# A top-256 search with eight rounds instead of nine, and both ends of its interval in one tile

## The chip, the core and the metric

The kernel runs on one core of one Trainium2 chip. The core has five engines that run side by side, each through its own fixed list of instructions: PE (TensorE, matmuls), DVE (VectorE), ACT (ScalarE), POOL (GpSimd) and SP (SyncE, which here issues the DMA transfers). The metric is the device time of one execution in microseconds (us); lower is better. The time before is the median of three runs, 2610.61 us (2607.62 to 2613.69).

## The reference

One decoder layer on 2048 tokens of width 1024. What matters here is how each query chooses its keys: an indexer scores all earlier positions, the 256 best are kept, and attention runs over these alone.

```python
rel = jax.nn.relu(jnp.einsum('bqhd,bsd->bqhs', qi_b.astype(jnp.float32), ki32))
score = jnp.einsum('bqhs,bqh->bqs', rel, w_b.astype(jnp.float32))
causal = key_pos[None, :] <= t_b[:, None]
score = jnp.where(causal[None], score, NEG_INF)
_, sel = lax.top_k(score, k_sel)
valid = sel <= t_b[None, :, None]
...
logits = jnp.where(valid[:, None], logits, NEG_INF)
p = jax.nn.softmax(logits, axis=-1).astype(v.dtype)
```

Around it stand one input projection, a short gated convolution (y = B * conv3(C * h)), RMS norms, one output projection, layer norms, and a SwiGLU feed-forward of width 2816.

## The kernel before, in words

The 2048 tokens are 16 blocks of 128. Blocks 0 and 1 have at most 256 earlier positions, so they take all; blocks 2 to 15 each need a threshold per query. The kernel finds it without sorting, in `topk`: it keeps an interval from `lo` to `hi` around the threshold of each query, guesses `t` inside it, counts how many scores are at or above `t`, and lets the count replace one end. `NITER` rounds of this bring the upper end to where between 248 and 255 scores lie above it; then one pass masks these, `V.max` takes the eight largest of the rest, and the missing rank picks the threshold (L549 to L555). The last pass (L559) writes the 0/1 mask `u` and counts it into `flag`. If any query's count is not exactly 256, a branch at the end of attention runs the general path: `general_topk` (31 bitwise rounds for every block) and attention once more.

A round is: for each block of the group, ACT counts the last `n2` columns with a sign activation (L507) and DVE counts the rest with a comparison that accumulates (L509); then small DVE instructions of 2 to 8 elements a row join the counts (L512), decide which end moves (L513 to L516), and interpolate the next `t` (L519 to L534; L536 to L541 are special steps of rounds 2 and 3). Counts and thresholds lie side by side in one tile `tcur`, as they do in `lo` and `hi`, so one predicated copy moves both.

The searches run in five groups. Blocks (2,3,4,5), (6,7,8) and (9,10) are the early ones. Their steps are interleaved with the scoring of further blocks (`weighted`, L454), with the projections, the convolution (`conv`, L732 on PE) and the weights of the adaLN modulation (L266). A group's search starts only when the group before it has ended. Scores of all blocks are written to memory (`s_d`). When scoring is over and the third search has ended, the memory it held is given to attention: query loads (`qst`, L838), scaled output weights (`wr`, L812), and the tile `scb` into which scores of the late groups (11,12,13) and (14,15) are loaded back. The late searches then run in the background of attention: one step of them in each step of attention. Attention takes blocks in the order 2, 4, 7, 0, 10, 1, 9, 3, 8, 5, 6, 11, 13, 12, 15, 14. For each block DVE first finds the largest logit per query and head (`maxima`: matmul L858, L860 on DVE, transpose L870 on PE), then PE makes logits (L883 to L885), ACT exponentials (L889, L890), GpSimd a rest (L891), and PE multiplies with the values (L901 to L903). GpSimd computes nothing in the front but small copies and memsets: the convolution's two-column halo (L740, L742) and the constants `zero` and `below`.

Every engine's list is fixed when the program is built: a scheduler orders the instructions by priority and by its own estimate of when each could start.

Of the kernel before, what the change touches and what calls it, by code (L numbers as in the profile page):

```python
# [11 lines left out]
F32 = mybir.dt.float32  # L12
F16 = mybir.dt.float16
BF16 = mybir.dt.bfloat16
I32 = mybir.dt.int32
AF = mybir.ActivationFunctionType
ALU = mybir.AluOpType
# [4 lines left out]
P = 128  # L22
# [29 lines left out]


TGT = 252.0
NITER = 9
CLIP = 0.04
PROBE = 2
DVE_SHARE = 0.42
# [67 lines left out]
def rsqrt(V, pool, dst, src, eps):  # L126
    n = dst.shape[1]
    v = pool.tile([P, n], F32, tag=f"rv{n}", name="rv", bufs=2)
    y = pool.tile([P, n], F32, tag=f"ry{n}", name="ry", bufs=2)
    a = pool.tile([P, n], F32, tag=f"rw{n}", name="rw", bufs=2)  # L130
    i = pool.tile([P, n], I32, tag=f"ri{n}", name="ri", bufs=2)
    V.tensor_scalar(v, src, eps, None, op0=ALU.add)
    V.tensor_scalar(i, v.bitcast(I32), 1, None, op0=ALU.logical_shift_right)
    V.tensor_scalar(y.bitcast(I32), i, -1.0, float(0x5F3759DF), op0=ALU.mult, op1=ALU.add)
    V.tensor_scalar(v, v, -0.5, None, op0=ALU.mult)
    for k in range(3):
        V.tensor_tensor(a, y, y, op=ALU.mult)
        V.tensor_tensor(a, a, v, op=ALU.mult)
        V.scalar_tensor_tensor(dst if k == 2 else y, a, 1.5, y, op0=ALU.add, op1=ALU.mult)
# [3 lines left out]
def body(ctx: ExitStack, tc: tile.TileContext, A, out, force=False):  # L143
    nc = tc.nc
    V, S_, G, T = nc.vector, nc.scalar, nc.gpsimd, nc.tensor
# [182 lines left out]
    for q in range(4):  # L328
# [5 lines left out]
        for b, ps in first.items():  # L334
            hi, lo = hts[b // 4]
# [18 lines left out]
    tk = tks.enter_context(tc.tile_pool(name="tk", bufs=1, side="right", reuse_waits="tile"))  # L354
# [103 lines left out]
    def topk(blocks, scs):  # L458
        nb = len(blocks)
        b0 = blocks[0]  # L460

        def sm(name, k=1):
            return tk.tile([P, k, nb], F32, tag=f"{name}", name=f"{name}{b0}", bufs=2)

        def cst(c):
            return ct[:, c + b0:c + b0 + nb]

        st6 = tk.tile([P, nb, 6], F32, tag="st6", name=f"st6_{b0}")
        mv = tk.tile([P, nb, 2], F32, tag="mv", name=f"mv_{b0}")
        for i in range(nb):  # L470
            m = 2 * TOPK if blocks[i] >= 4 else TOPK
            head = tk.tile([P, 2 * TOPK], F32, tag="sp", name="head")[:, 0:m]
            S_.activation(head, scs[i][:, 0:m], AF.Copy, scale=1.0 / SS2)
            V.bn_stats(st6[:, i], head)
            V.bn_aggr(mv[:, i], st6[:, i])
            yield
        mu, sd = sm("mu")[:, 0], sm("sd")[:, 0]
        rsqrt(V, tk, sd, mv[:, :, 1], 1e-30)
        V.scalar_tensor_tensor(sd, sd, SS2, mv[:, :, 1], op0=ALU.mult, op1=ALU.mult)
        V.tensor_scalar(mu, mv[:, :, 0], SS2, None, op0=ALU.mult)  # L480
        tcur, lo, hi = sm("tc", 2), sm("lo", 2), sm("hi", 2)
        a, f = sm("a")[:, 0], sm("f")[:, 0]
        big, nbig = sm("big"), sm("nbig")
        cd, ca2 = sm("cd")[:, 0], sm("ca2")[:, 0]
        t = tcur[:, 0]
        cnt = tcur[:, 1]
        V.tensor_tensor(a, sd, cst(C_Z), op=ALU.mult)
        V.tensor_tensor(t, a, mu, op=ALU.add)
        V.scalar_tensor_tensor(lo[:, 0], sd, -6.0, mu, op0=ALU.mult, op1=ALU.add)
        V.scalar_tensor_tensor(hi[:, 0], sd, 8.0, mu, op0=ALU.mult, op1=ALU.add)  # L490
        zero, below = sm("zero")[:, 0], sm("below")[:, 0]

        n2 = int(sum(b + 1 for b in blocks) / nb * P * (1 - DVE_SHARE)) // 64 * 64
        big_at, tgt = TOPK - n2 / 2.0, TGT - n2 / 2.0
        V.tensor_scalar(lo[:, 1], cst(C_N), -n2 / 2.0, None, op0=ALU.add)
        V.memset(hi[:, 1], -n2 / 2.0)
        G.memset(zero, 0.0)
        G.memset(below, -2100.0)
        dd = sm("dd", 2)
        yield  # L500
        for it in range(NITER):
            for i, b in enumerate(blocks):
                n = (b + 1) * P
                n1 = n - n2
                j1 = tk.tile([P, 1024], BF16, tag="j1", name="j1", bufs=1)
                j2 = tk.tile([P, 1216], BF16, tag="j2", name="j2", bufs=1)
                S_.activation(j2[:, 0:n2], scs[i][:, n1:n], AF.Sign, bias=t[:, i:i + 1],  # L507
                              scale=-1.0, accum_out=ca2[:, i:i + 1])
                V.tensor_scalar(j1[:, 0:n1], scs[i][:, 0:n1], t[:, i:i + 1], None,  # L509
                                op0=ALU.is_ge, op1=ALU.add, accum_out=cd[:, i:i + 1])  # L510
                yield
            V.scalar_tensor_tensor(cnt, ca2, -0.5, cd, op0=ALU.mult, op1=ALU.add)  # L512
            V.tensor_scalar(big[:, 0], cnt, big_at, None, op0=ALU.is_ge)  # L513
            V.tensor_scalar(nbig[:, 0], cnt, big_at, None, op0=ALU.is_lt)
            V.copy_predicated(lo, big.bitcast(I32).broadcast_to([P, 2, nb]), tcur)
            V.copy_predicated(hi, nbig.bitcast(I32).broadcast_to([P, 2, nb]), tcur)  # L516
            if it == NITER - 1:
                break
            V.tensor_tensor(dd, hi, lo, op=ALU.subtract)  # L519
            d = dd[:, 0]  # L520
            if it == 0:
                V.scalar_tensor_tensor(a, cnt, -tgt, sd, op0=ALU.add, op1=ALU.mult)
                V.tensor_tensor(a, a, cst(C_SL), op=ALU.mult)
                V.tensor_tensor(a, a, t, op=ALU.add)
                V.scalar_tensor_tensor(f, d, 0.02, lo[:, 0], op0=ALU.mult, op1=ALU.add)
                V.tensor_tensor(a, a, f, op=ALU.max)
                V.scalar_tensor_tensor(f, d, -0.02, hi[:, 0], op0=ALU.mult, op1=ALU.add)
                V.tensor_tensor(t, a, f, op=ALU.min)
            else:
                V.reciprocal(a, dd[:, 1])  # L530
                V.scalar_tensor_tensor(f, lo[:, 1], -tgt, a, op0=ALU.add, op1=ALU.mult)
                V.tensor_scalar(f, f, CLIP - 1.0, -CLIP, op0=ALU.max, op1=ALU.min)
                V.tensor_tensor(f, f, d, op=ALU.mult)
                V.tensor_tensor(t, lo[:, 0], f, op=ALU.subtract)  # L534
            if it == PROBE:
                V.tensor_scalar(a, lo[:, 0], 0.0, None, op0=ALU.is_lt)  # L536
                V.scalar_tensor_tensor(f, hi[:, 0], 0.0, a, op0=ALU.is_gt, op1=ALU.mult)
                V.copy_predicated(t, f.bitcast(I32), zero)
            if it == PROBE + 1:
                V.tensor_scalar(f, hi[:, 0], 0.0, None, op0=ALU.is_equal)  # L540
                V.copy_predicated(t, f.bitcast(I32), below)  # L541
            yield
        r, thr, m8 = sm("rk")[:, 0], sm("thr")[:, 0], tk.tile([P, nb, 8], F32, tag="m8", name=f"m8{b0}")
        ri = tk.tile([P, nb], I32, tag="ri_", name=f"ri{b0}")
        V.tensor_scalar(ri, hi[:, 1], n2 / 2.0 + 0.25, None, op0=ALU.add)
        V.tensor_scalar(r, ri, -1.0, float(TOPK), op0=ALU.mult, op1=ALU.add)
        for i, b in enumerate(blocks):
            n = (b + 1) * P
            sp = tk.tile([P, S], F32, tag="sp", name="sp", bufs=1)  # L549
            V.tensor_scalar(sp[:, 0:n], scs[i], hi[:, 0, i:i + 1], 2.0 * NEG, op0=ALU.is_ge, op1=ALU.mult)  # L550
            V.tensor_tensor(sp[:, 0:n], sp[:, 0:n], scs[i], op=ALU.add)
            yield
            V.max(m8[:, i], sp[:, 0:n])
            pick = tk.tile([P, 8], F32, tag="pick", name="pick")
            V.scalar_tensor_tensor(pick, ct[:, C_IOTA:C_IOTA + 8], r[:, i:i + 1], m8[:, i], op0=ALU.is_equal,  # L555
                                   op1=ALU.mult, accum_out=thr[:, i:i + 1])
            yield
            u = tk.tile([P, S], BF16, tag="u", name="u", bufs=1)
            V.tensor_scalar(u[:, 0:n], scs[i], thr[:, i:i + 1], None, op0=ALU.is_lt, op1=ALU.add,  # L559
                            accum_out=flag[:, b:b + 1])  # L560
            S_.activation(u[:, 0:n], u[:, 0:n], AF.Copy, scale=NEG)
            dma(u_d[b - 2], u[:, 0:n])
            yield
# [1065 lines left out]
```

## Time and profile before

| | before |
|---|---|
| median of three runs | 2610.61 us |
| the profiled execution, time | 2611.21 us |
| its span | 2609.4 us |
| PE busy | 2346.9 us (90%) |
| DVE busy | 1868.2 us (72%) |
| ACT busy | 1197.2 us (46%) |
| POOL busy | 1179.2 us (45%) |
| mean granted PE clock | 0.952 |

The shares are means over stages that differ. Up to about 590 us the kernel projects, scores, convolves and runs the early searches; from there to about 1310 us it attends, with the late searches up to about 900 us; behind it the feed-forward, where PE is nearly always busy. What an edit to the search is worth has to be read from the first two stages.

### The profile page before, as it was taken

The page shows a single profiled execution, that of the slowest core. Times are in us where ns is not written, and L with a number is a line of the kernel's source. Part 1 is how long each engine was busy: PE and PEld are TensorE (multiplying, and loading weights), DVE is VectorE, ACT ScalarE, POOL GpSimd, SP SyncE. Part 2 cuts the span into 40 slices and gives each one's busy share as a digit, 9 for nine tenths or more (in the row PEclk, how much of TensorE's full clock was granted, in tenths as well). Part 3 has the DMA queues.
Part 4 walks back from the last instruction along what each step waited for, and adds up shares of the span by engine and source line. Part 5 has one row for each costly group of instructions (what it writes and reads, how often), then busy time and mean ns, then how long its engine had stood idle before and what let it go on. Part 6 is the DMA issues. An engine that isn't in the chain of part 4 may idle for free. (4 is left out here: it accounts for less than half of the span.)

```text
span 2609.4 us, 38313 instructions
## 1 busy us (share of the span) xinstructions
PE 2346.9 (90%) x13538; PEld 1128.6 (43%) x13538; DVE 1868.2 (72%) x3812; ACT 1197.2 (46%) x2291; POOL 1179.2 (45%) x950
## 2 busy tenths in 40 slices
PE   6799999895787889989969999999999996999998
PEld 3444444342443445545524444444444442344443
DVE  8998999989998977775268776666666787422223
ACT  3687767555676655757733332333323343110000
POOL 3000000004453564676636655655556664855445
PEclk8899999997898989999989999999999997999999
DMA  7421442415121142330133222222222236444443
GB/s 265 129 99 68 147 135 90 148 57 188 47 97 63 64 147 71 112 127 30 67 122 121 85 69 81 73 77 85 78 84 85 89 101 195 150 137 146 134 133 122
DMA packets 213913, 281.69 MB, mean 108 GB/s; under 512 B 15824, under 2 KB 128848, under 8 KB 212944
## 3 DMA queue, kind: packets, MB, share of 16 engines
q1 hardware_dynamic: 213712, 279.17, 33.7%
q8 instruction: 107, 1.75, 0.3%
q14 instruction: 94, 0.77, 0.1%
HBM read 183.20 MB, written 95.91 MB: 107 GB/s over the span
## 5 line engine op out<-in xcount | busy, mean ns | idle before, releaser
L1201 PE MATMUL f<-h,wwg 128*128 128x512 f16 x1800 | 419.0, 383 | 24.5 <-ACT h L1164 18.1
L891 POOL TENSOR_TENSOR pr<-p,ph 128x512 f16<-128x512 f32 x272 | 326.2, 1218 | 222.9 <-ACT ph L890 147.6
L1201 PE MATMUL f<-h,wwu 128*128 128x512 f16 x1800 | 413.4, 379 | 0.0
L1497 PEld LDWEIGHTS <-gi 128*128 128x128 f16 x1848 | 181.6, 99 | 276.7 <-DMA gi<-gg_d 46.3
L1235 POOL TENSOR_TENSOR go<-g,go 128x512 f16<-128x512 f32 x126 | 169.6, 1356 | 275.3 <-ACT go L1234 233.6
L1201 PEld LDWEIGHTS <-wwg 128*128 128x128 f16 x1848 | 181.9, 99 | 231.3 <-issue 13.7
L1201 PEld LDWEIGHTS <-wwu 128*128 128x128 f16 x1848 | 180.8, 98 | 233.1 <-issue 15.6
L1497 PE MATMUL f<-wdo,gi 128*128 128x512 f16 x1032 | 243.2, 388 | 15.3 <-DMA gi<-gg_d 8.5
L860 DVE CUSTOM_DVE_ANT_0 jk<-m,ua 128x512 bf16<-128x512 f32 (+3 forms) x320 | 193.9, 606 | 64.6 <-PE m L858 49.7
L889 ACT ACTIVATE p<-l 128x512 f32<-128x512 f32 x272 | 157.6, 597 | 87.2 <-PE l L885 77.4
L1234 ACT ACTIVATE go<-g 128x512 f16<-128x512 f32 x132 | 82.7, 628 | 231.6 <-issue 82.8
L447 ACT ACTIVATE r<-xs 128x512 f32<-128x512 f32 (+3 forms) x304 | 154.0, 549 | 60.8 <-PE xs L446 16.6
L890 ACT ACTIVATE ph<-p 128x512 f16<-128x512 f32 x272 | 166.1, 633 | 3.3 <-PE o L903 0.8
L1497 PE MATMUL f<-wdr,gi 128*128 128x512 f16 x576 | 137.1, 387 | 14.4 <-DMA gi<-gg_d 14.4
L732 PE MATMUL b<-hi,wch 128*128 128x512 f16 x384 | 147.0, 383 | 1.2 <-ACT g L737 1.2
L732 PE MATMUL b<-lo,wch 128*128 128x512 f16 x384 | 146.8, 382 | 0.0
L732 PE MATMUL b<-hi,wcl 128*128 128x512 f16 x384 | 146.3, 381 | 0.0
L903 PE MATMUL o<-vst,pr 128*128 128x65 f16 x1088 | 136.9, 198 | 6.8 <-POOL pr L891 6.4
L901 PE MATMUL o<-vst,ph 128*128 128x65 f16 x1088 | 140.1, 196 | 1.2 <-ACT ph L890 1.0
L902 PE MATMUL o<-vst,ph 128*128 128x64 f16 x1088 | 139.5, 196 | 0.0
L858 PE MATMUL m<-k1T,qst 128*128 128x512 f16 (+3 forms) x320 | 110.1, 376 | 32.1 <-DVE mp L860 26.1
L1464 ACT ACTIVATE frs<-fmv,epsw 128x1 f32<-128x1 f32 x16 | 4.7, 295 | 283.3 <-DVE fmv L1461 283.3
(384 smaller groups left out, 5319.8 us busy)
## 6 DMA issues: line engine op xcount, KB each, us to landing
gg_d<-go SPq DMA_DIRECT2D x154, 256.0 KB, 2.6
gi<-gg_d SPq DMA_DIRECT2D x112, 256.0 KB, 3.0
wa<-in_w_ada SPq DMA_DIRECT2D x64, 256.0 KB, 2.9
wg<-in_wg SPq DMA_DIRECT2D x49, 256.0 KB, 3.0
wu<-in_wu SPq DMA_DIRECT2D x49, 256.0 KB, 3.0
wd<-in_wd SPq DMA_DIRECT2D x44, 256.0 KB, 2.9
gi<-gg_d SPq DMA_DIRECT2D x56, 192.0 KB, 2.8
wa<-in_w_ada SPq DMA_DIRECT2D x16, 512.0 KB, 8.6
```

The lines of the kernel that those rows point to most:

```text
L447: S_.activation(r[:, i:i + e], ps[:, 0:e], AF.Relu)
L732: T.matmul(ps, w[:, k, j * P:(j + 1) * P], x[:, k], start=n == 0, stop=n == 3 * KT - 1)
L860: V.tensor_tensor_reduce(jk[:, 0:w], ps[:, 0:w], u[:, j * 512:j * 512 + w], scale=1.0, scalar=-3e38, op0=ALU.add, op1=ALU.max, accum_out=m ...
L889: S_.activation(p32, pl_, AF.Exp, scale=DH ** -0.5)
L890: S_.activation(ph, p32, AF.Copy)
L891: G.tensor_tensor(pr, p32, ph, op=ALU.subtract)
L901: T.matmul(o, lhs, vst[:, kt, 64:129], start=kt == 0 and hh == 0, stop=False)
L902: T.matmul(o[:, 0:64], lhs, vst[:, kt, 0:64], start=False, stop=False)
L903: T.matmul(o, pr[:, hh * P:(hh + 1) * P], vst[:, kt, 64:129], start=False, stop=kt == b and hh == 3)
L1201: T.matmul(ps, w[:, x, k * P:(k + 1) * P], h[:, y, :, k], start=n == 0, stop=n == 11)
L1235: (V if (p, grp) in LASTG else G).tensor_tensor(o[:, :, 1], x4, o[:, :, 0], op=ALU.subtract)
L1497: T.matmul(ps, g[:, p - p0, x], wd_tiles[m, p][:, y], start=p == 0 and n == 0, stop=p == NP - 1 and n == 2)
```

## The change

`NITER` goes from 9 to 8. `lo` and `hi` become two halves of one tile `ends`. Where two comparisons made the predicates `big` and `nbig` and two predicated copies moved `lo` and `hi`, one comparison now makes both predicates at once (the count is at or above the goal, compared with a constant row of 0 for `lo` and of 1 for `hi`), and one predicated copy moves whichever end it is. The constant tile `upper` is written by two GpSimd memsets at the start of each group.

```diff
-NITER = 9
+NITER = 8
...
-        tcur, lo, hi = sm("tc", 2), sm("lo", 2), sm("hi", 2)
+        tcur = sm("tc", 2)
+
+        ends = tk.tile([P, 2, 2, nb], F32, tag="ends", name=f"ends{b0}", bufs=2)
+        lo, hi = ends[:, 0], ends[:, 1]
         a, f = sm("a")[:, 0], sm("f")[:, 0]
-        big, nbig = sm("big"), sm("nbig")
+        which, upper = sm("which", 2), sm("upper", 2)
...
+        G.memset(upper[:, 0], 0.0)
+        G.memset(upper[:, 1], 1.0)
...
             V.scalar_tensor_tensor(cnt, ca2, -0.5, cd, op0=ALU.mult, op1=ALU.add)
-            V.tensor_scalar(big[:, 0], cnt, big_at, None, op0=ALU.is_ge)
-            V.tensor_scalar(nbig[:, 0], cnt, big_at, None, op0=ALU.is_lt)
-            V.copy_predicated(lo, big.bitcast(I32).broadcast_to([P, 2, nb]), tcur)
-            V.copy_predicated(hi, nbig.bitcast(I32).broadcast_to([P, 2, nb]), tcur)
+            V.scalar_tensor_tensor(which, tcur[:, 1:2].broadcast_to([P, 2, nb]), big_at, upper,
+                                   op0=ALU.is_ge, op1=ALU.not_equal)
+            V.copy_predicated(ends, which.bitcast(I32).unsqueeze(2).broadcast_to([P, 2, 2, nb]),
+                              tcur.unsqueeze(1).broadcast_to([P, 2, 2, nb]))
```

The change also moves other instructions, since the scheduler orders anew. Three places, where a name with a number is one buffer of that tile, and where L517 to L524 of the changed kernel are L512 to L519 of the one before, L737 is L732, L817 is L812, and L863 and L865 are L858 and L860.

DVE, one of the last rounds of the third search, before:

```order
L512 SCALAR_TENSOR_TENSOR tc_3300<-ca_3308,cd_3307 128x2
L513 TENSOR_SCALAR big_3305<-tc_3300 128x2
L514 TENSOR_SCALAR nbig_3306<-tc_3300 128x2
L515 COPY_PREDICATED lo_3301<-big_3305,tc_3300 128x4
L516 COPY_PREDICATED hi_3302<-nbig_3306,tc_3300 128x4
L519 TENSOR_TENSOR dd_3319<-hi_3302,lo_3301 128x4
L530 RECIPROCAL a_3303<-dd_3319 128x2
```

and now:

```order
L517 SCALAR_TENSOR_TENSOR tc_3127<-ca_3134,cd_3133 128x2
L518 SCALAR_TENSOR_TENSOR which_3131<-tc_3127,upper_3132 128x4
L520 COPY_PREDICATED ends_3128<-which_3131,tc_3127 128x8
L524 TENSOR_TENSOR dd_3147<-ends_3128 128x4
L535 RECIPROCAL a_3129<-dd_3147 128x2
```

Four instructions became two; each of the five now needs the result of the one ahead of it. In all, DVE has 149 instructions fewer.

DVE, the end of scoring (`scl` are scores of blocks 11 to 15, L620 is the last step of scoring, `ada` the adaLN weights), before:

```order
L454 SCALAR_TENSOR_TENSOR scl_3934<-r,wis,scl_3934 128x1024
L755 TENSOR_TENSOR y<-y,g 128x512
L475 BN_AGGR mv_3251<-st_9_3250 128x2
L620 TENSOR_TENSOR scl_3934<-scl_3934,ct 128x128
L132 TENSOR_SCALAR rv<-mv_3251 128x2
```

and now:

```order
L514 TENSOR_SCALAR j_3153,cd_3133<-sc_2399,tc_3127 128x512
L266 SCALAR_TENSOR_TENSOR ada_6043<-wa,ca,ada_6043 128x512
L751 SCALAR_TENSOR_TENSOR y<-u,pp,y 128x512
L454 SCALAR_TENSOR_TENSOR scl_3820<-r,wis,scl_3820 128x1024
L514 TENSOR_SCALAR j_3226,cd_3133<-sc_2399,tc_3127 128x640
L753 SCALAR_TENSOR_TENSOR y<-b,y 128x512
```

The head of the third search and the counts of its first round (L514 of the changed kernel) moved ahead of the last scores; before, they stood behind them. From the last score to the search's last instruction there are 189 DVE rows before and 128 now.

PE, the seam between convolution and attention, before:

```order
L732 LDWEIGHTS wcl_5974
L732 MATMUL b<-hi_1062,wcl_5974 128x512
L858 LDWEIGHTS qst_6674
L858 MATMUL m<-k1T,qst_6674 128x384
```

and now:

```order
L737 LDWEIGHTS wch_5859
L737 MATMUL b<-lo_1063,wch_5859 128x512
L863 LDWEIGHTS qst_6560
L863 MATMUL m<-k1T,qst_6560 128x384
...
L737 LDWEIGHTS wcl_5860
L737 MATMUL b<-hi_1062,wcl_5860 128x512
```

Before, the convolution's last matmul stands ahead of the first matmul of attention. Now 67 convolution matmuls stand behind that first one, mixed with the maxima of the first block.

## Rows read from the trace of the kernel before

**Rows 1.** Stretches: busy us (count) of PE, PEld, DVE, ACT, POOL; PE clock.

```profile
183.00:590.00 407.00, 392.35 (x1865) 181.76 (x1863) 380.00 (x985) 270.89 (x550) 20.27 (x41) 0.99 0.33 106
590.00:900.00 310.00, 232.22 (x1923) 123.08 (x1922) 293.28 (x822) 202.36 (x399) 135.24 (x116) 0.87 0.27 93
...
480.00:520.00 40.00, 33.38 (x138) 14.10 (x136) 39.65 (x79) 21.25 (x35) 2.95 (x4) 0.96 0.42 138
520.00:580.00 60.00, 60.00 (x269) 27.15 (x268) 53.56 (x176) 30.19 (x55) 1.52 (x10) 1.00 0.15 45
580.00:600.00 20.00, 11.11 (x49) 4.67 (x47) 14.92 (x33) 7.61 (x11) 0.19 (x1) 0.90 0.86 297
```

**Rows 2.** Waits of PE, 590 to 900 us: total us, times, longest.

```profile
PE m L858 <- DVE mp L860: 19.4, 29, 2.2
PE m L870 <- DVE mx L866: 16.4, 4, 6.2
```

**Rows 3.** Waits of DVE, 590 to 900 us.

```profile
DVE jk L860 <- PE m L858: 5.3, 5, 1.8
```

**Rows 4.** Waits of PE, 183 to 590 us.

```profile
PE xs L446 <- ACT r L447: 6.2, 6, 2.0
PE b L752 <- ACT g L749: 5.8, 3, 4.3
```

**Rows 5.** The chain that ended last, its first pieces: start, us, what.

```profile
1336.38 4.46 PE f L1201 x12
```

**Rows 6.** Line L509 alone by stretch: length, DVE busy us (count), PE clock.

```profile
183.00:590.00 407.00, 50.69 (x162) 0.99 0.33 106
590.00:900.00 310.00, 46.33 (x90) 0.87 0.27 93
```

**Rows 7.** Tile `big` (L513 and L515) by stretch, columns as before.

```profile
183.00:590.00 407.00, 9.10 (x54) 0.99 0.33 106
590.00:900.00 310.00, 9.69 (x36) 0.87 0.27 93
```

**Rows 8.** Tile `nbig` (L514 and L516) by stretch.

```profile
183.00:590.00 407.00, 8.85 (x54) 0.99 0.33 106
590.00:900.00 310.00, 9.58 (x36) 0.87 0.27 93
```

**Rows 9.** Timeline of DVE, a round of the third search: start, us, instruction.

```profile
557.58 0.16 DVE L512 SCALAR_TENSOR_TENSOR tc<-ca,cd 128x2 f32<-128x2 f32 x1 [0.41 <-ACT j L507]
557.78 0.17 DVE L513 TENSOR_SCALAR big<-tc 128x2 f32<-128x2 f32 x1
557.86 0.16 DVE L514 TENSOR_SCALAR nbig<-tc 128x2 f32<-128x2 f32 x1
...
558.45 0.17 DVE L530 RECIPROCAL a<-dd 128x2 f32<-128x2 f32 x1
558.65 0.16 DVE L531 SCALAR_TENSOR_TENSOR f<-lo,a 128x2 f32<-128x2 f32 x1
...
559.45 0.75 DVE L509 TENSOR_SCALAR_CACHE_REDUCE j<-sc,tc 128x512 bf16<-128x512 f32 x1
560.12 0.09 DVE L509 DVE_READ_ACCUMULATOR j<-sc,tc 128x1 f32 x1
...
561.96 0.16 DVE L512 SCALAR_TENSOR_TENSOR tc<-ca,cd 128x2 f32<-128x2 f32 x1 [0.84 <-ACT j L507]
```

**Rows 10.** Timeline of DVE: scoring's end, the third search's first round, its end.

```profile
512.55 0.28 DVE L620 TENSOR_TENSOR scl<-scl,ct 128x128 f32<-128x128 f32 x1
...
521.80 0.15 DVE L512 SCALAR_TENSOR_TENSOR tc<-ca,cd 128x2 f32<-128x2 f32 x1
...
583.20 0.08 DVE L559 DVE_READ_ACCUMULATOR u<-sc,thr 128x1 f32 x1
```

**Rows 11.** Timeline of SP's queue and PE at the seam.

```profile
582.28 0.63 SPq L838 DMA_DIRECT2D qst<-q_d  x1
...
587.37 0.81 PE L858 MATMUL m<-k1T,qst 128*128 128x384 f16 x4
...
600.54 0.40 PE L870 MATMUL m<-ct,mx 128*72 128x128 f32 x1 [8.44 <-DVE mv L475]
```

**Rows 12.** Line L515: ns min/median/max, first and last start, forms.

```profile
L515 DVE COPY_PREDICATED lo<-big,tc x45: 152/167/1134, 193.5 to 885.3; 128x6 f32<-128x6 int32 x18, 128x4 f32<-128x4 int32 x18, 128x8 f32<-128x8 int32 x9
```

## The prediction

> **What bounds the kernel now.** Start with the table of stretches [rows 1], because the change touches only 183 to 900 us and a mean over the whole kernel hides two regimes. From 183 to 590 us (projections, scores, convolution, and the three early searches) PE is busy 392.4 of 407 us and DVE 380.0: both are nearly full. From 590 to 900 us (attention with the two late searches in its background) DVE is busy 293.3 of 310 us, PE only 232.2, and PE's granted clock is down to 0.87. Next come the waits: between 590 and 900 us PE's longest are for the maxima that DVE takes [rows 2], while DVE waits for PE only 5.3 us [rows 3]. So DVE sets the pace there. In the front PE waits 12.0 us for two results of ACT [rows 4], and by the code each of them follows a DVE step (L454, L748). The chain that ended last begins at 1336 us [rows 5], after all this, so it can't price the change. I use it for one thing: it is made of work and of loads that follow work, so what is won before it is kept as a shift.
>
> **One search round on DVE.** The timeline of the last early search shows a bare round: 561.96 - 557.58 = 4.38 us from one L512 to the next [rows 9]. Instructions that depend on each other start 0.20 us apart; independent neighbours start 0.08 us apart although each is recorded with 0.16. So a small instruction takes 0.075 us of DVE when other work fills the gaps, and up to 0.20 when nothing does.
>
> **Term 1, the count passes.** Their line, accumulator reads included, is busy 50.7 us in the front and 46.3 us behind it, over nine rounds [rows 6]. One round of all early groups is 5.6 us, of all late groups 5.1 us; less the overlap in the records (0.07 us for 9 and 5 passes) 5.0 and 4.8 us. ACT loses its part of the count too; it is busy 202 of 310 us in the late stretch [rows 1], so that is worth nothing by itself.
>
> **Term 2, the small instructions.** A removed round takes eleven with it. Each of the remaining rounds (24 early, 16 late) loses two: L513 to L516 become one comparison and one predicated copy. In the front the four lines are busy 9.10 + 8.85 us [rows 7, 8], 0.166 each, none waiting. Late they are 9.69 + 9.58 us for only 72, 0.27 each. The Trainium skill, "SBUF — State Buffer", section "SBUF: two separate sides", says that DVE and GpSimd share a port pair as an exclusive lock which a DVE instruction with two SBUF inputs, or in a two-port mode, waits for. That agrees with 0.166 against 0.27, and it speaks against part of the change: the new comparison reads two SBUF tiles where the old ones read one, so the waits might only move to it; by that the late saving is the lower end below.
>
> Late round removed: eleven small ones at 0.075 (all hidden) to 0.27 each; I take 0.18, or 2.0 us a group, 4.0 for both groups (1.6 to 5.9). With the passes 8.8 us (6.4 to 10.7). Two instructions fewer in 16 rounds: 2.4 us at 0.075; at the measured late mean 0.54 a round less 0.17 of overlap, 5.9 us. I take 4, since a GpSimd instruction that no longer meets L515 may meet the next one. Late sum on DVE 12.8 us (8.8 to 16.6). DVE is busy 95% of that stretch, so I turn 0.9 of it into time: **11.5 us**, ends 7 and 16.6.
>
> **Term 3, the front up to the end of scoring (183 to 512 us).** Groups (2,3,4,5) and (6,7,8) lose a round each: 3.4 us of passes and 2 x 0.83 of small ones; two instructions in 16 rounds at 0.075 are 2.4 us: 7.5 us of DVE. But the order of the changed kernel moves work in: the head of the third search and its first round now stand ahead of the last score, about 27 small instructions, two BN_STATS and two passes, 4.7 us of DVE. What is left is 2.8 us. PE has little to win: 6.6 us idle from 480 to 520 us, where DVE is at 39.65 of 40 [rows 1]. I take **3 us**, between 0 (PE is the bound) and 7 (the crunch at 480 to 520 goes). The two new memsets per group go to GpSimd, idle here 387 of 407 us [rows 1]. The halo copies that the convolution needs (L740, L742) queue behind them. They wait for nothing: the buffer is that of the group two before, whose search has ended. So I cost them at nothing; if one did wait, a halo copy and with it PE would wait as long.
>
> **Term 4, the seam at 583 to 600 us.** Attention's first loads wait for the memory that the third search holds. Before: scoring ends at 512.55, the search's last instruction is at 583.20 [rows 10], the first query load is issued at 582.28, PE starts the first maxima at 587.37, when the last convolution matmul is in, and then stands idle 8.44 us until 600.54 [rows 11]. From 580 to 600 us DVE is idle 5.1 us and PE 8.9 [rows 1]. After: from the end of scoring to the end of the search there are 128 DVE rows instead of 189. In time that is 70.7 us, less a round of 4.4, less 0.8 for the two instructions in seven rounds, less 9.3 (512.55 to 521.80, head and first round, now earlier [rows 10]): about 56 us, so the search ends 14.5 us earlier against the convolution, whose PE work is unchanged. The order agrees: the first maxima matmul now stands 67 convolution matmuls before their end, and at 60.0/269 us each [rows 1] that is 14.9 us. The burst of loads and the first maxima then run beside convolution. DVE's own saving here is 3.0 us for the round and 0.8; to that come the idle time at the seam (up to 5.1), and the 6.4 us that DVE is idle from 520 to 580 [rows 1], of which the 14 us window can refill only a part. I take **10 us**; the ends are 4 (own work alone) and 15 (all of it).
>
> **Sum.** 11.5 + 3 + 10 = 24.5 us. Against the profiled execution of 2611.2 us (its span is 2609.4) that gives 2586.7; the median of the runs shown is 0.6 us lower, so 2586. The ends together: 7 + 0 + 4 = 11 and 16.6 + 7 + 15 = 38.6, hence 2600 and 2572.
>
> **Rivals.** *PE takes over.* With the maxima earlier, PE's own work could become the bound in part of 590 to 900 us and keep half of the gain, 2599. For it: 232 us of matmuls at a granted clock of 0.87. Against it: some 36 us of its idle time (19.4 and 16.4) name DVE's maxima alone [rows 2].
>
> *The seam backfires.* PE runs in order, and 67 convolution matmuls now queue behind the first maxima. If the search ends as late against the convolution as before, PE stands still for up to 14.9 us and convolution with it: 24.5 less the seam's 10 and 14.9 more lost, 2611. It decides when u of the last block lands later than PE's arrival there. Against it: the 14.5 us above, worked out without that order, cover it.
>
> *The wide copy is dear (slower).* No row shows a predicated copy with both its inputs broadcast, on up to 16 elements. The nearest, L515, has 0.167 us as its median for 4, 6 and 8 elements alike, and 1.13 us at its longest [rows 12]. If every one of the 40 new copies cost that longest, they would take 40 x 0.97 = 39 us more on DVE, and the time would be 2586 + 39 = 2625. It decides at 0.61 us more per copy (24.5/40). The equal medians for three sizes speak against it.
>
> *Eight rounds don't settle a row.* Then the flag (L559) sends the kernel through the general path: 31 passes over 17,024 columns at 0.75/512 us each [rows 9], 770 us, and attention a second time, some 700 us (590 us to the chain's start at 1336 [rows 5] bounds it): about 4,060 us. A single row of the 1,792 decides. Following the search's arithmetic in single precision on the reference's inputs, one row is open after seven rounds, none after eight or nine; so this is remote, though the margin is one round.
>
> **How the numbers follow.** Forecast 0.68; PE takes over 0.16; the seam backfires 0.06; dear copy 0.04; general path 0.02; more than my upper ends (PE's clock rises as its gaps close, 0.87 in the late stretch) 0.04. The range 2568 to 2603 holds the forecast with its ends, PE taking over, and a little of the last; it leaves out about 2 in 10 with the tails of each. A measurement of this kernel can tell about 0.2%, 5.2 us, from no change. Faster by more than that: 0.68 + 0.16 + 0.04 and some of the seam case, 0.89. Within it: 0.05, most of the seam case. Slower: 0.06.
>
> **What would show it.** The profile after should have 112 passes on the count line instead of 126 and 149 DVE instructions fewer; 590 to about 876 us with DVE still near 95%; the third search ending at least 10 us before the last convolution matmul; no PE wait of 8 us at the first transpose of maxima; everything behind 1000 us shifted by one constant. I am wrong if the new copy is recorded above 0.3 us in the front, if PE idles inside the convolution for the first query tile, or if DVE's share from 590 to 900 us drops while the time does not.

## The result and the profile after

The changed kernel takes **2589.45 us** (median of four runs, 2585.36 to 2590.99) against 2609.11 us for the kernel before beside it: a ratio of 0.9916 [0.9903, 0.993], 20 to 22 us faster. The profiled execution is the shortest of its four, 2585.36 us, 25.9 us below the profiled 2611.21 of before. So the forecast of 2586 held in its sum. It did not hold in its parts, and most of what follows is about that.

First the stretches of the kernel after, with the columns of [rows 1]: length, busy us (count) of PE, PEld (PE's weight loads), DVE, ACT, POOL, then PE's granted clock, the DMA share and GB/s.

```profile
183.00:590.00 407.00, 392.09 (x1871) 182.27 (x1869) 382.81 (x927) 269.16 (x543) 22.54 (x50) 0.98 0.37 119
590.00:900.00 310.00, 236.84 (x1882) 124.99 (x1883) 287.58 (x753) 202.09 (x398) 151.62 (x122) 0.86 0.28 93
...
480.00:520.00 40.00, 40.00 (x179) 18.16 (x178) 37.74 (x82) 22.13 (x41) 3.08 (x4) 1.00 0.48 154
520.00:580.00 60.00, 60.00 (x274) 27.37 (x273) 51.26 (x139) 29.35 (x49) 1.64 (x12) 1.00 0.36 128
580.00:600.00 20.00, 9.09 (x29) 3.30 (x28) 19.00 (x48) 9.04 (x15) 3.54 (x4) 0.72 0.29 93
```

PE's idle time at the end of scoring is gone: from 480 to 520 us it is busy 40.0 us where it was busy 33.38 [rows 1]. From 590 to 900 us DVE is 5.7 us less busy, PE 4.6 us more. At the seam, 580 to 600 us, PE is busy 9.09 us, less than the 11.11 of [rows 1].

PE's waits from 590 to 900 us (total us, times, longest), which answer to [rows 2]:

```profile
PE m L863 <- DVE mp L865: 20.3, 23, 2.2
PE l L888 <- ACT p L894: 14.0, 15, 4.6
PE m L964 <- DVE z L956: 12.2, 4, 4.7
PE m L875 <- DVE mx L871: 8.8, 4, 3.2
```

The wait for the transposed maxima fell from 16.4 to 8.8 us; the one for the single maxima stayed (19.4, now 20.3).

The seam in the timelines of DVE, SP's queue and PE (start, us, instruction, idle before), answering to [rows 10, 11]:

```profile
559.53 0.08 DVE L564 DVE_READ_ACCUMULATOR u<-sc,thr 128x1 f32 x1
...
555.46 1.08 SPq L843 DMA_DIRECT2D qst<-q_d  x1
...
582.00 0.38 PE L737 MATMUL b<-hi,wcl 128*128 128x512 f16 x1
583.60 0.22 PE L863 MATMUL m<-k1T,qst 128*128 128x128 f16 x1 [1.23 <-ACT pc L877]
587.64 0.59 PE L863 MATMUL m<-k1T,qst 128*128 128x512 f16 x1 [3.83 <-DVE mp L865]
589.32 0.27 PE L863 MATMUL m<-k1T,qst 128*128 128x128 f16 x1 [1.09 <-DVE mp L865]
591.25 2.08 PE L757 MATMUL b<-g,ct 128*128 128x512 f32 x2 [1.66 <-ACT g L754]
```

The third search ends at 559.53, 23.7 us earlier than the 583.20 of [rows 10], and 22 us ahead of the last convolution matmul at 582.00. Query loads are issued at 555.46 instead of 582.28 [rows 11]. The single wait of 8.44 us is gone, but several of 1 to 4 us stand in its place.

What was saved on DVE, by line and stretch (length, DVE busy us, count): the count passes L514, answering to [rows 6], and the new pair, L518 and L520, answering to [rows 7, 8] (tile `which`).

```profile
183.00:590.00 407.00, 44.81 (x144) 0.98 0.37 119
590.00:900.00 310.00, 41.13 (x80) 0.86 0.28 93
...
183.00:590.00 407.00, 7.92 (x48) 0.98 0.37 119
590.00:900.00 310.00, 10.76 (x32) 0.86 0.28 93
...
L520 DVE COPY_PREDICATED ends<-which,tc x40: 158/170/1087, 193.3 to 830.8; 128x12 f32<-128x12 int32 x16, 128x8 f32<-128x8 int32 x16, 128x16 f32<-128x16 int32 x8
```

There are 72 + 40 = 112 passes (their accumulator reads double the count in the rows), as forecast. The new pair is recorded at 0.33 us a round in the front and 0.67 in the late stretch, where the four old lines took 17.95/27 = 0.66 and 19.27/18 = 1.07 [rows 7, 8]. The new copy has 0.170 us as its median, the old one 0.167 [rows 12].

GpSimd in the front, where the new memsets of `upper` stand (L502), shows one thing that the prediction had otherwise:

```profile
235.72 0.10 POOL L502 MEMSET upper<- 128x2 f32 x1 [19.79 <-DVE which L518]
259.27 0.11 POOL L725 MEMSET halo<- 128x8 f32 x1 [23.42 <-DVE qq L431]
422.46 0.10 POOL L502 MEMSET upper<- 128x3 f32 x1 [14.50 <-DVE which L518]
425.01 1.11 POOL L747 COPY halo<-u 128x2 f32<-128x2 f32 x1 [2.41 <-DVE u L746]
```

Three of these memsets did wait for a search's last comparison, 35.0 us in all. The halo instruction behind each of them then waited on for DVE all the same (23.4, 2.4 and 15.5 us).

### The profile page after: what moved, and what is told of

Its sections match the earlier page's. It is cut to its first block, busy times and chain, and to the rows that moved or that the text cites. A ratio compares the mean times of both kernels' runs of the same rounds, so it can differ in the third digit from the quotient of the medians.

```text
span 2583.5 us, 38131 instructions
## 1 busy us (share of the span) xinstructions
PE 2335.9 (90%) x13538; PEld 1126.0 (44%) x13538; DVE 1835.4 (71%) x3649; ACT 1185.9 (46%) x2263; POOL 1184.6 (46%) x960
## 5 line engine op out<-in xcount | busy, mean ns | idle before, releaser
L1502 PEld LDWEIGHTS <-gi 128*128 128x128 f16 x1848 | 181.5, 99 | 276.1 <-DMA gi<-gg_d 44.8
L1206 PEld LDWEIGHTS <-wwg 128*128 128x128 f16 x1848 | 181.8, 99 | 232.0 <-issue 14.1
L865 DVE CUSTOM_DVE_ANT_0 jk<-m,ua 128x512 bf16<-128x512 f32 (+3 forms) x320 | 193.7, 605 | 71.9 <-PE m L863 56.1
L1502 PE MATMUL f<-wdr,gi 128*128 128x512 f16 x576 | 136.8, 386 | 16.7 <-DVE g L1213 8.8
L737 PE MATMUL b<-hi,wch 128*128 128x512 f16 x384 | 146.8, 382 | 0.0
L737 PE MATMUL b<-lo,wch 128*128 128x512 f16 x384 | 146.6, 382 | 0.0
L737 PE MATMUL b<-hi,wcl 128*128 128x512 f16 x384 | 146.3, 381 | 0.0
L863 PE MATMUL m<-k1T,qst 128*128 128x512 f16 (+3 forms) x320 | 109.2, 372 | 35.6 <-DVE mp L865 31.5
```

The source lines that it names most:

```text
L737: T.matmul(ps, w[:, k, j * P:(j + 1) * P], x[:, k], start=n == 0, stop=n == 3 * KT - 1)
L865: V.tensor_tensor_reduce(jk[:, 0:w], ps[:, 0:w], u[:, j * 512:j * 512 + w], scale=1.0, scalar=-3e38, op0=ALU.add, op1=ALU.max, accum_out=m ...
L1206: T.matmul(ps, w[:, x, k * P:(k + 1) * P], h[:, y, :, k], start=n == 0, stop=n == 11)
L1502: T.matmul(ps, g[:, p - p0, x], wd_tiles[m, p][:, y], start=p == 0 and n == 0, stop=p == NP - 1 and n == 2)
```

## Experiments

Two theories stood at the start. **The conversion:** DVE sets the pace wherever it is 95% busy, so each us of DVE work removed from the late stretch is worth about a us; this carried the largest term of the forecast. **The chain:** DVE's share there is no bound; what counts is how soon the three early searches, one behind the other, come to their end, since attention's first loads and DVE's preparations wait for that. All ratios are to the kernel before on the same chip, with 95% intervals; us are worked out as the difference of ratios times 2611.

### The parts apart

Eight rounds, with the old two comparisons and two copies:

```diff
 (before)
-NITER = 9
+NITER = 8
```

> Eight rounds, but lo and hi in two tiles with two comparisons and two predicated copies as before. By the terms of the prediction (A): a round less is worth about 1 us in the front, 9 us at the seam (63 of 67 convolution matmuls still stand behind the first maxima) and 8 us late, so about 2591 us, 0.993 of before. If instead the small instructions and their waits for GpSimd carry the late gain (B), a round less alone gives no more than 10 us, 2599.

Measured 2587.23 us, 0.9905 [0.9891, 0.9919], below both numbers. With eight rounds everywhere the old instructions are no slower than the new (0.9916): the new comparison and copy add nothing that can be seen to the round removed.

Nine rounds with the new tile, comparison and copy:

```diff
 (after)
-NITER = 8
+NITER = 9
```

> Nine rounds, but one tile, one comparison and one predicated copy as after. By the terms (A): 27 early rounds and 18 late ones lose two small instructions, worth about 2 us in the front and at the seam (10 convolution matmuls behind the first maxima, not 67) and 4 us late, so about 2603 us. If the waits for GpSimd only move to the next instruction (B): 2607, not to be told from before. If the new copy were dear (C): 2615 or more.

Measured 2602.44 us, 0.9968 [0.9957, 0.998]. Alone, the new pair is worth 8.4 us: the dear copy does not exist. The expected 2603 is met, but not shown in its parts: 2 us early and 4 late were put, and the third search alone ends 7.4 us earlier.

Eight rounds in the early groups and nine in the late ones, and the reverse:

```diff
 (after; the second kernel has 9 and 8 exchanged)
+        rounds = 8 if b0 < LATE[0][0] else 9
-        for it in range(NITER):
+        for it in range(rounds):
...
-            if it == NITER - 1:
+            if it == rounds - 1:
```

> The changed kernel, but nine rounds in the two late groups and eight in the three early ones. By the terms (A): the front and the seam keep their 13 us and the late stretch keeps only the two instructions in 18 rounds, 3.6 us: about 2592 us. If the late stretch is bound elsewhere (B), a late round more costs nothing and this is as fast as the changed kernel, 2589.

> The changed kernel, but nine rounds in the three early groups and eight in the two late ones. By the terms (A): the late 11.5 us stay, at the front and seam only some 2 us (10 convolution matmuls behind the first maxima): about 2596 us. If the late round is worth nothing (B): 2603, as with the copy alone.

Measured 2586.27 us, 0.9905 [0.9892, 0.9918], with the early round gone, and 2603.41 us, 0.9969 [0.9957, 0.9981], with the late round gone. The late round is worth **nothing** that can be seen beside nine early rounds (0.9969 against 0.9968) and nothing beside eight (0.9916 against 0.9905, overlapping, the wrong way if at all); the intervals leave room for some 4 us in the first pair and 2 in the second, not for the 8 that the prediction's terms gave it. The early round is worth 0.9968 - 0.9905 = 16.4 us in the one pair and 0.9969 - 0.9916 = 13.8 in the other. That is twice the DVE work in it, some 7 us (5.0 of passes by [rows 6], and nine small instructions in each of three groups at about 0.08). So the conversion falls, in both pairs.

### Doubling instead of removing

After, with each late count pass on DVE made twice, and then each early one (the result of both passes is the same number):

```diff
 (after; the second kernel has "b0 < LATE[0][0]")
+                for _ in range(2 if b0 >= LATE[0][0] else 1):
                     V.tensor_scalar(j1[:, 0:n1], scs[i][:, 0:n1], t[:, i:i + 1], None,
```

> The changed kernel with each DVE count pass of the two late groups done twice (the second writes the same values): 40 passes, 38 us more of DVE between 600 and 900 us. If DVE sets the pace there (D, the prediction's term), 0.9 of it shows: about 2623 us. If the stretch is bound by the attention of PE, ACT and GpSimd over its whole length and the search only shares DVE's gaps (L), 0 to 10 us show: 2590 to 2600.

> The changed kernel with each DVE count pass of the three early groups done twice: 72 passes, about 40 us more of DVE before 580 us, all of it also in the serial chain of the searches. No convolution matmul is left behind the first maxima. If the length of the search chain decides when attention starts (S), the seam's gain goes and more: 2610 to 2630 us. If the front is bound by PE alone (P), it stays near 2589.

Late: 2605.55 us, 0.9972 [0.9959, 0.9985], 14.6 us above the kernel after. The recorded passes grow from 41.13 to 82.33 us: 41 us of DVE time, or 38 if each of the 40 overlaps its neighbour by 0.07 us. That is 0.36 to 0.38 us of time for each us of DVE work, with DVE busy 297.63 of 310 us. It lies between the two expectations, nearer to the second.

```profile
590.00:900.00 310.00, 82.33 (x160) 0.87 0.23 76
...
590.00:900.00 310.00, 231.91 (x1924) 124.89 (x1924) 297.63 (x802) 193.46 (x379) 128.62 (x113) 0.87 0.23 76
```

The rows are the pass line alone and then all engines, from 590 to 900 us, with the columns as before.

Early: 2625.61 us, 1.0042 [1.0029, 1.0055], 32.9 us above the kernel after, for passes recorded 44.8 us longer (89.63 against 44.81): 0.73 us for each us of DVE work. Timelines of PE and DVE at its seam, and the stretch behind it:

```profile
576.08 0.38 PE L738 MATMUL b<-hi,wcl 128*128 128x512 f16 x1
...
609.05 1.46 PE L864 MATMUL m<-k1T,qst 128*128 128x384 f16 x4 [29.71 <-DMA qst<-q_d]
...
609.46 0.08 DVE L565 DVE_READ_ACCUMULATOR u<-sc,thr 128x1 f32 x1
...
580.00:625.00 45.00, 6.33 (x19) 2.50 (x20) 37.66 (x95) 12.29 (x21) 2.77 (x6) 0.50 0.56 182
```

This shows the chain at its plainest. The convolution ends at 576 us, the third search at 609, and PE stands idle 29.7 us for the first query load, which goes into memory that the search holds; SP issues it only at 605.78. In 45 us PE works 6.33, at a granted clock of 0.50, the lower of its two levels (1.2 of 2.4 GHz).

### One early group, and fewer early rounds

Eight rounds in the third search alone, nine elsewhere:

```diff
 (after)
+        rounds = 8 if b0 == GROUPS[2][0] else 9
```

> The copy and comparison of the changed kernel, eight rounds in the third search alone, nine in all others; 48 convolution matmuls stand behind the first maxima (10 with nine rounds everywhere, 67 with eight in all early groups). If what counts is how much earlier the third search ends against the convolution (S), the gain goes with that number: of the 16 us between nine and eight early rounds some 11 come, about 2592 us. If DVE's busy time counts (D), the round saves 3 us: 2599.

Measured 2599.66 us, 0.9946 [0.9929, 0.9963], 5.7 us better than nine rounds everywhere with the same instructions; its search ends 4.9 us earlier. That is less than the 11 us that S had put by the place among the convolution's matmuls, and nearer to the 3 us of D; but the time moved as far as the search's end did. So the last group is not special: most of the early round's 14 to 16 us came from the two groups ahead of it, whose work lies further from the seam.

Seven rounds early, eight late:

```diff
 (after)
+        rounds = 7 if b0 < LATE[0][0] else 8
```

> Seven rounds in the three early groups, eight in the late ones; followed in single precision on these inputs, no row of blocks 2 to 10 is open after seven rounds, so the flag stays down. 120 convolution matmuls stand behind the first maxima. If an earlier end of the search keeps paying (S), another 8 to 16 us: 2574 to 2582. If the seam's idle time is used up (U), only DVE's 8 us of work or less show: 2582 to 2589.

Measured **2574.66 us, 0.9854 [0.9834, 0.9875]**: another 16.2 us for another early round. This beats both kernels. On these inputs no row of blocks 2 to 10 is left open; on others one may be, and the next run but one has the price of that.

Seven rounds early, nine late:

```diff
 (after)
+        rounds = 7 if b0 < LATE[0][0] else 9
```

> Seven rounds in the early groups, nine in the late ones. If a late round is worth nothing (L), as fast as seven early and eight late, 0.985 of before, about 2575 us. If late rounds count at all when the seam is no longer the longest wait (D), 6 to 10 us more than that: 2581 to 2585.

Measured 2586.51 us, 0.9906 [0.9893, 0.9919], above every number expected. Here a late round does cost time: 13.6 us more than with eight. So "a late round is free" holds with eight and nine early rounds, and not with seven.

Seven rounds everywhere:

```diff
 (after)
-NITER = 8
+NITER = 7
```

> Seven rounds in all five groups. Followed in single precision on these inputs, one row of block 11 is open after seven rounds, so its count is not 256, the flag is up and the general path runs. The prediction's price for that rival was 770 us of bitwise rounds and some 700 us of attention: about 4050 us. If the row settles on the chip after all, it is near 2575.

Measured 5059.86 us, in a single execution: the general path runs, by the author's arithmetic for one open row of block 11. It is 1,000 us dearer than the 4,050 expected. Rows of its stretches (columns as before) and of the general path's pass:

```profile
600.00:1200.00 600.00, 508.33 (x4734) 285.85 (x4734) 490.10 (x1191) 397.53 (x799) 358.30 (x298) 0.94 0.27 90
...
1300.00:2420.00 1120.00, 22.91 (x126) 10.98 (x127) 1024.16 (x2364) 9.25 (x17) 9.18 (x10) 0.50 0.04 13
2420.00:3700.00 1280.00, 885.21 (x4878) 421.26 (x4877) 338.95 (x957) 396.94 (x740) 337.69 (x292) 0.60 0.10 33
3700.00:5058.00 1358.00, 1272.07 (x5922) 572.46 (x5919) 760.04 (x945) 375.26 (x645) 760.54 (x550) 0.96 0.34 103
...
L1575 DVE TENSOR_SCALAR_CACHE_REDUCE gj<-gs,cand 128x384 f32<-128x384 f32 (+13 forms) x434 | 641.9, 1479 | 15.6
```

The 434 passes (31 for each of 14 blocks) take 641.9 us of the general path's 1,120, less than the 770 worked out for them; the small instructions around each pass and the rest take the other 478. The second attention takes some 1,360 us from its first exponential to its last (2393.4 to 3751.8), where the kernel before takes 692 (604.5 to 1296.4); in its bulk the granted clock is 0.60. It is also built otherwise: called without the pool that the first one is given, `attention` runs with `keep, lag, pb_` of 1, 0, 1 instead of 3, 2, 5 (one buffer for the exponentials instead of five), and from 2420 to 3700 us PE waits again and again for the rest that GpSimd makes:

```profile
PE o L908 <- POOL pr L896: 102.1, 231, 1.1
```

In the first attention, from 600 to 1200 us, that wait is 6.7 us. How much of the second one's length comes from the buffers and how much from the clock was not tried.

### The copy beside eight early rounds, and a collision

The old comparisons and copies with eight rounds early and nine late:

```diff
 (before)
+        rounds = 8 if b0 < LATE[0][0] else 9
```

> The kernel before with eight rounds in the early groups and nine late, and two comparisons and two copies as before. If the copy's late gain of 4 to 6 us (from 666 us to the end of attention, before 630.0 us, nine rounds with the new copy 625.3) stands by itself (A), 4 to 6 us above the same rounds with the new copy (0.9905 of before): 0.9925. If it is swallowed as the late round is (L): 0.9905.

Measured 2591.96 us, 0.9924 [0.991, 0.9937], against 0.9905 with the new pair: some 5 us, but the intervals overlap. With the first experiment (no gain at 8 and 8) the worth of the new pair once the round is gone is between nothing and 5 us.

Last, a suspicion from the trace (a block begins, here and below, at its first exponential). In the kernel after, the late search frees its memory so early that the feed-forward's first weight preparation on GpSimd starts at 870.5 us, and what the attention block needs stands behind it:

```profile
870.50 1.65 POOL L1092 TENSOR_TENSOR wg<-wg,wg 128x512 f32<-128x512 f32 x1 [15.47 <-DMA wg<-in_wg]
872.08 0.15 POOL L869 MEMSET mx<- 128x64 f32 x1
872.19 1.63 POOL L1092 TENSOR_TENSOR wu<-wu,wu 128x512 f32<-128x512 f32 x1
873.89 2.22 POOL L878 TENSOR_TENSOR q<-pc,ct 8x1024 f16<-8x1024 f32 x1
```

GpSimd waits 15.5 us for a weight load while the memset of the next maxima queues behind. The block in the ninth place begins at 888.5 us, 1.6 us *later* than before (886.9), though the block in the fourth place begins 21.6 us earlier (683.5 against 705.1). Did this eat the late gain? An experiment holds the search's memory until that block is done, with six small DVE instructions added:

```diff
 (after; the places where `lasts` takes the search's tiles are left out)
+HOLD = 8
...
+                    if background is not None and pp_ == HOLD:
+                        hold = ap.tile([P, 2], F32, tag="hold", name="hold", bufs=1)
+                        V.tensor_copy(hold[:, 0:1], on_[:, 0, 0:1])
+                    if background is not None and pp_ == 11:
+                        for x in lasts.values():
+                            V.scalar_tensor_tensor(hold[:, 1:2], x[:, 0:1], 1.0, hold[:, 0:1], op0=ALU.mult, op1=ALU.add)
```

> The changed kernel, with the memory that the late searches used held by six small DVE instructions until attention has finished the block at place 8 in its order, so that the preparation of the first feed-forward weights can't move up behind the search's earlier end and stand in GpSimd's queue ahead of attention's work. If that collision (15.5 us of GpSimd waiting for wg, and place 8 starting 24 us later than with nine late rounds) eats the late round's gain (K), 5 to 10 us come back: 2580 to 2585. If the work only changes places and the stretch as a whole is bound (W), it stays at 2589; above 2595 if the preparation then comes too late.

Measured 2587.88 us, 0.9916 [0.9902, 0.993], the same as without. GpSimd's timeline shows the collision gone, the preparation behind the memsets now:

```profile
869.66 0.15 POOL L874 MEMSET mx<- 128x64 f32 x1 [14.65 <-PE m L880]
...
941.86 1.27 POOL L1103 TENSOR_TENSOR wg<-wg,wg 128x512 f32<-128x512 f32 x1 [0.63 <-DVE wwg L217]
```

The blocks in the ninth to eleventh places do begin 5.6 to 8.7 us earlier than in the kernel after (the ninth at 882.9), but the twelfth begins at 991.4 against 991.9. The suspicion falls: the collision delayed three blocks and cost nothing that the time shows.

### All runs on one line

The end of the third search in each profiled execution, and the measured time, as shifts against before (583.20 us, ratio 1); the run that took the general path is left out:

| kernel (rounds early / late) | end of third search, us | shift, us | time by the ratio, us |
|---|---|---|---|
| early passes doubled (8/8) | 609.46 | +26.3 | +11.0 |
| 9/8, new pair | 576.12 | -7.1 | -8.1 |
| 9/9, new pair | 575.81 | -7.4 | -8.4 |
| third search 8, else 9 | 570.96 | -12.2 | -14.1 |
| 8/9, old pair | 560.93 | -22.3 | -19.8 |
| 8/8, old pair | 559.60 | -23.6 | -24.8 |
| **after, 8/8** | 559.53 | -23.7 | -21.9 |
| 8/9, new pair | 558.04 | -25.2 | -24.8 |
| 8/8, memory held | 556.93 | -26.3 | -21.9 |
| 7/8, new pair | 548.82 | -34.4 | -38.1 |
| late passes doubled (8/8) | 559.04 | -24.2 | -7.3 |
| 7/9, new pair | 549.21 | -34.0 | -24.5 |

From the second row to the tenth the time follows the search's end nearly one for one, within 4.4 us. In most of these the early work changed along with the end, and no run was built to move the end alone. The two last rows have more late work than the early lead leaves room for, and the first row is a delay of which part is covered.

## Why the prediction was right, and where it was not

**The sum** was 24.5 us off the profiled execution; that execution moved by 25.9, the medians by 19.7, the ratio says 21.9. The number is right by luck: two errors of opposite sign, some 11 us too much late and some 7 to 10 too little at the seam, nearly cancel.

**Late, 11.5 us (7 to 16.6): measured about nothing.** The work was sized well. Late passes fell by 46.33 - 41.13 = 5.2 us recorded, where the step put 5.1 [rows 6]. For the small ones, 0.40 us a round fewer were recorded for the pair (1.07 - 0.67); over 16 rounds, less 0.17 of overlap in each, that is 3.7 us against the 4 taken. The lock weighed there ("SBUF — State Buffer", section "SBUF: two separate sides", the Trainium skill) agrees with the trace: every late small instruction of a round that is recorded above 0.3 us ends 0.01 to 0.03 us after a GpSimd instruction does. One from before and one from after, each with the GpSimd instruction beside it:

```profile
704.40 1.13 DVE L514 TENSOR_SCALAR nbig<-tc 128x3 f32<-128x3 f32 x1
704.35 1.16 POOL L891 TENSOR_TENSOR pr<-p,ph 128x512 f16<-128x512 f32 x1 [0.42 <-ACT ph L890]
...
829.87 0.87 DVE L518 SCALAR_TENSOR_TENSOR which<-tc,upper 128x4 f32<-128x4 f32 x1
829.57 1.16 POOL L896 TENSOR_TENSOR pr<-p,ph 128x512 f16<-128x512 f32 x1 [5.30 <-ACT ph L895]
```

But the argument that the old comparisons, reading one SBUF tile, were better off does not hold: L514, which reads one, is recorded at 5.80/18 = 0.32 us in the late stretch (L513 at 3.29/18 = 0.18), the new one at 5.94/16 = 0.37. The step that failed is "I turn 0.9 of it into time". Three measurements stand against it: 0.9969 against 0.9968, 0.9916 against 0.9905, and at most 0.38 us per us in the doubled passes. The first two try the late round, some 9 of the 12.8 us; the new pair's late part, 4 us, was tried only together with its early part. The late search did end earlier, its last instruction by 54 us (911.60 to 857.31), and the time did not follow. The text had named the sign: DVE's share from 590 to 900 us drops (293.28 to 287.58) while the time does not. A share of 95% says that DVE had something to do, not that the end waited for all of it. Where the time went can be seen in part. Stretches of the kernel after, and below them of the one with nine late rounds and eight early:

```profile
800.00:900.00 100.00, 76.38 (x610) 40.60 (x609) 89.15 (x189) 63.60 (x127) 61.87 (x46) 0.86 0.32 105
900.00:1000.00 100.00, 92.39 (x856) 52.62 (x855) 71.59 (x178) 60.88 (x129) 53.75 (x48) 0.97 0.26 87
...
800.00:900.00 100.00, 84.09 (x780) 47.39 (x779) 95.70 (x235) 67.79 (x132) 52.62 (x42) 0.95 0.25 82
900.00:1000.00 100.00, 81.92 (x676) 44.85 (x673) 83.00 (x176) 56.32 (x123) 61.63 (x49) 0.91 0.32 104
```

Without the late round PE does less from 800 to 900 us and makes up for it in the next hundred: 168.8 us of matmuls against 166.0 over both. The granted clock is lower first and higher then (0.93 in both from 600 to 1300 us). The work changes places; why PE did not use the time that DVE had free was not settled.

**Front, 3 us (0 to 7): the convolution's last matmul moved by 5.2** (587.2 to 582.0), and scoring's end by 9. Inside its range; the 6.6 us of PE idle from 480 to 520 us did go [rows 1]. The border to the seam is blurred: eleven matmuls of the first maxima, 2.8 us of PE, now stand ahead of that last one, so up to some 3 us may be moved from the seam to the front. One premise was wrong without harm: the memsets of `upper` did not "wait for nothing", they waited 35.0 us; but the halo instruction behind each was held up by DVE anyway, so the cost was nothing, as put.

**Seam, 10 us (4 to 15): measured about 17 to 20.** The early part as a whole, by the kernel with nine late rounds, is 24.8 us; less the front's 5.2 this leaves 19.6, and 16.7 by the kernel after, both above the upper end. The mechanism was named rightly: loads issued 27 us earlier, the first maxima under the convolution, and from scoring's end to the search's end 56.0 us (503.5 to 559.5), where 56 had been worked out. The size came from DVE's own saving plus its idle time from 520 to 600 us. That was the mis-sized term, and for a reason: the idle time at the seam did not close (PE busy 9.09 of 20 us), yet the gain came. It shows behind the seam: the first exponential comes only 3.8 us earlier (604.5 to 600.7), the block in the second place begins 6.9 us earlier, the one in the third 18.6 (666.4 to 647.9, single executions). DVE scales the output weights from 570.5 to 614.4 us instead of 593.2 to 643.0, partly under the convolution, and PE then finds its maxima earlier. From 600 to 700 us:

```profile
600.00:700.00 100.00, 68.15 (x499) 33.46 (x500) 97.27 (x288) 61.63 (x118) 43.30 (x37) 0.76 0.27 86
```

```profile
600.00:700.00 100.00, 80.18 (x658) 42.47 (x658) 95.47 (x293) 69.57 (x140) 48.93 (x44) 0.87 0.27 85
```

The first is before, the second after: 499 matmuls against 658 with DVE about equally busy. That the early chain sets this is shown by the runs that lengthen and shorten it; that it acts through the weight scaling is read from the timelines and was not tried by itself.

**"Everything behind 1000 us shifted by one constant"** held roughly: the blocks in the twelfth to sixteenth places begin 19.5 to 23.2 us earlier, the last exponential 24.9 us. On the way it did not hold: the block in the ninth place shows no lead at all.

**Rivals.** *PE takes over* (2599) did not happen: PE's wait for its maxima stayed, and the medians lie 10 us below. *The seam backfires* did not happen here. With the early passes doubled PE stood idle 29.7 us for the load, but there no convolution matmul was queued behind the maxima, so the rival's own form was seen in no run. *The dear copy* is refuted by 0.170 us in the median and by the 8.4 us gained with it alone. *The general path* did not run at eight rounds; with seven it does, and costs 2,449 us more than the kernel before, where 1,450 had been worked out: the passes were sized from above, but the small instructions around them and the second attention's length were missed.

**Left open.** With seven early rounds a late round costs 13.6 us, and with eight or nine nothing. In both seven-round kernels the third search ends at the same time (548.82 and 549.21), so the difference arises behind it. The scheduler lays out attention anew each time; which of the moved instructions does it was not settled. It is also open how the lead that is missing at the ninth place comes back by the twelfth; the collision on GpSimd accounts for 5.6 us of it. Where the middle blocks begin says little about the end: with eight early and nine late rounds the ninth begins at 861.9, 26.6 us ahead of the kernel after, and the last exponentials come at 1270.4 and 1271.5.

## What to carry to other kernels

An engine at 95% in a stretch is a suspect, not the bound: double its work there before you price a saving, for here some 40 us more cost 15, and some 8 us less gave nothing. Look instead for the serial chain whose end opens something (here memory for the next stage's loads): a round in that chain held some 7 us of work and was worth 14 to 16, and the time followed its end nearly one for one in nine kernels. And where a scheduler orders anew, parts measured alone need not add: 8.4 us for the new pair became 0 to 5 once the round was gone.

## What was not expected of the hardware

The second attention of the general path runs at a mean granted clock of 0.60, although PE is busy 885 of the 1,280 us read, while the first attention of the same execution has 0.94 with 508 of 600. Ahead of it lies the general path, 1,120 us in which PE was busy 22.9 us, at 0.50. The two attentions are not alike in their buffers nor in what runs beside them, so what keeps the clock near its lower level (1.2 of 2.4 GHz) for so long is not shown; that it was low there is. The 0.50 in the 45 us behind the convolution of the doubled early passes, where PE worked 6.3 us, is like that of the general path: in both PE had almost nothing to do.
